# Gate and up of a feed-forward block, from weights stationary to tokens stationary

## The chip, the cores and the metric

One core of a Trainium2 chip runs the whole program. The metric is the device time of one execution in microseconds (us); lower is better. Before the change three timed executions took 2022.8, 2023.21 and 2023.25 us, median 2023.21. A profiled execution beside them took 2023.11 us.

The core has a matrix engine (TensorE, PE in the profile; its weight loads are listed apart as PEld), a vector engine (VectorE, DVE), a scalar engine for activation functions and copies (ScalarE, ACT), GpSimd (POOL) and SyncE (SP), which here does nothing but issue DMAs. Each engine works through its own list of instructions in order, and waits on semaphores where it needs another engine's or a DMA's result. Matrix products accumulate in PSUM banks of 128 partitions x 512 fp32; everything else lies in SBUF.

## What is computed

One sequence of 256 tokens, width 2048, in fp32, passes through two blocks: a sliding-window attention block, and a block with latent attention, differential attention, gates and a feed-forward part. The change touches the feed-forward part, at the end:

```python
h2 = rmsnorm_2(x, ffn_norm_g[i])
x = x + (jax.nn.silu(h2 @ w_ffn_gate[i]) * (h2 @ w_ffn_up[i])) @ w_ffn_down[i]
return rmsnorm_2(x, final_norm_g)
```

`w_ffn_gate` and `w_ffn_up` are 2048 x 5632, `w_ffn_down` is 5632 x 2048.

## The kernel before

**Weights.** All weights lie in HBM as 340 chunks of 16 tiles of 128 x 128, in the order in which the program takes them. SP loads a chunk (1 MB) into one of four buffers `w_raw` (line 53). Half a chunk, 8 tiles, is then cut (lines 79 to 85): ACT casts it to fp32r (`w_hi`), DVE subtracts that from the original (`w_lo`). `w_hi` and `w_lo` have four buffers each. A product is made of three parts: high x high, high x low and low x high. A chunk's load waits until both halves of the chunk four before it have been cut, and a cut until PE is done with the half four before it.

**Two forms of a product.** Activations stand feature-major: 16 tiles `h3_k` of 128 features, each with 256 tokens of high part and 256 of low part side by side. In `gemm` (line 319) a weight tile is stationary and the activations stream: one matmul 512 wide with `w_hi` (high and low part at once, to two halves of a bank), one 256 wide with `w_lo`. The result is feature-major, and its two halves have to be added (`total`, line 387: an ACT copy and a DVE addition). In `gemm_nat` (line 375, with `nat3`, line 367) 128 tokens of an activation tile are stationary and 512 columns of weights stream: three matmuls 512 wide for each of the two token halves, for four weight tiles. The result has the tokens on the partitions, and is complete in one bank. Before the change `gemm_nat` is used for the values of the two attentions (`uv`, `dv`) and for `down`.

**Feed-forward before.** For each of 44 column tiles of gate and of up (lines 958 to 971) `gemm` runs over 16 k. The gate result is multiplied by the tokens' scale `rb` (the reciprocal root mean square, broadcast over the partitions by `rows`, line 282, with a PE matmul), Silu runs on ACT, the up result is multiplied in, and the product is split into `act{m}`, which is the stationary operand of `down`. The first two column tiles of gate and up run interleaved (`gemm4`). `down` then takes `act` in the order of k, 44 of them for each of four column blocks of 512 (the last block has its last eight k held back).

**What runs between.** `after_out` (line 939) is a generator, stepped by `between` after every 16 weight tiles: it makes the scale `r_3`, broadcasts it, and turns the residual `x2` from feature-major to token-major (`x2n`, eight tiles of 128 tokens x 512 features): four PE transposes and one ACT copy per tile (lines 949 to 953). `x2n` is read after the first column block of `down`.

**Buffers and order.** Activations, products and temporaries share one pool, `unit`, of 67 tiles of 128 x 512. A scheduler orders the instructions of each engine ahead of time; a buffer that is given out again makes the new writer wait for the old readers. DMAs of SP, and those of POOL, go round eight completion semaphores each, and a DMA waits for the one eight before it.

Of the kernel before, what the change touches and what calls it, by code (L numbers as in the profile page):

```python
# [9 lines left out]
F32 = mybir.dt.float32  # L10
F32R = mybir.dt.float32r
AF = mybir.ActivationFunctionType
ALU = mybir.AluOpType

P = 128
S = 256
D = 2048
KD = D // P
DFF = 5632
KF = DFF // P  # L20
# [150 lines left out]
def block_kernel(ctx, tc, order, w, x01, xt, bc, fg, cst, out):  # L171
    nc = tc.nc
# [9 lines left out]
    def unit(name, dt=F32):  # L182
        return up.tile([P, 512], dt, name=name, tag="u", bufs=NU)
# [4 lines left out]
    def bank(tag):  # L188
        return psum.tile([P, 512], F32, name=f"ps_{tag}", tag=tag, bufs={"g": 4, "s": 2, "t": 2}[tag])
# [10 lines left out]
    def tt(o, a, b, op):  # L200
        nc.vector.tensor_tensor(out=o, in0=a, in1=b, op=op)  # L201
# [28 lines left out]
    def split_scaled(src, g, hl):  # L230

        hi = hl[:, 0:S]
        if g is None:
            a = nc.scalar.copy(out=hi, in_=src)
            b = nc.vector.tensor_tensor(out=hl[:, S:], in0=src, in1=hi.bitcast(F32), op=ALU.subtract)
        else:
            a = nc.scalar.activation(out=hi, in_=src, func=AF.Copy, scale=g)
            b = nc.vector.scalar_tensor_tensor(out=hl[:, S:], in0=src, scalar=g, in1=hi.bitcast(F32),
                                               op0=ALU.mult, op1=ALU.subtract)
        return a, b  # L240
# [41 lines left out]
    def rows(r, rb=None):  # L282

        dg = unit("diag")[:, 0:S]
        for tb in range(2):
            nc.vector.tensor_scalar(out=dg[:, tb * P:tb * P + P], in0=ident, scalar1=r[:, tb:tb + 1], scalar2=None,
                                    op0=ALU.mult)
        ps = bank("t")
        mm(ps[:, 0:S], ones, dg, True, True)
        if rb is not None:  # L290
            nc.vector.tensor_copy(out=rb, in_=ps[:, 0:S])
        return ps[:, 0:S]
# [26 lines left out]
    def gemm(name, m, acts, tag="g"):  # L319

        ps = bank(tag)
        parts = [(ps, W.take(name, k * P, m * P), acts[k]) for k in range(len(acts))]
        if len(parts) > HALF:
            runs(parts[:HALF], parts[HALF:], HALF)
        else:
            runs(parts, [], len(parts))
        return ps

    def gemm4(name, ms, acts):

        pp = [bank("g"), bank("g"), bank("s"), bank("s")]
        opened = set()
        for k in range(len(acts)):
            parts = [(pp[j], W.take(name, k * P, m * P), acts[k]) for j, m in enumerate(ms)]
            same, other = ("hi", "lo") if k % 2 == 0 else ("lo", "hi")
            run(same, parts, opened)
            run(other, parts, opened)
            between.tiles(len(parts))
        return pp
# [26 lines left out]

    def nat3(o, hl, tb, hi, lo, first, last):

        xh = hl[:, tb * P:tb * P + P]
        xl = hl[:, S + tb * P:S + tb * P + P]  # L370
        mm(o, xh, hi, first, False)
        mm(o, xh, lo, False, False)
        mm(o, xl, hi, False, last)
# [13 lines left out]
    def total(o, ps):  # L387

        nc.scalar.copy(out=o, in_=ps[:, S:])  # L389
        tt(o, o, ps[:, 0:S], ALU.add)  # L390

    def scaled(o, ps, rb):
        total(o, ps)
        tt(o, o, rb, ALU.mult)
# [24 lines left out]
    def transposed(p, on_act=False):  # L419

        ps = bank("t")
        for j in range(3):
            nc.tensor.transpose(out=ps[:, j * P:j * P + P], in_=p[:, j * P:j * P + P], identity=ident)  # L423
        pt = unit("prob_t")[:, 0:384]
        if on_act:
            nc.scalar.copy(out=pt, in_=ps[:, 0:384])
        else:
            nc.vector.tensor_copy(out=pt, in_=ps[:, 0:384])
        return pt


    sq = Squares(8)
# [7 lines left out]
    h = Lazy(KD, first_h)  # L440
# [135 lines left out]
    g = []  # L576
# [348 lines left out]
    h = []  # L925
    for m, ps in blocks("out", 0, 16, mg):
# [5 lines left out]
        split_scaled(t, gcol(G_FFN, m), hl)  # L932
        h.append(hl)
        sq.add(t)
    rb = unit("rb_3")[:, 0:S]
    r_3 = const.tile([P, 2], F32, name="r_3")
    x2n = []

    def after_out():
        yield  # L940
        nc.vector.tensor_copy(out=r_3, in_=rstd(sq.sums(), D))
        yield
        rows(r_3, rb)
        for cb in range(4):
            for tb in range(2):
                yield
                ps = bank("t")
                for i in range(4):
                    nc.tensor.transpose(out=ps[:, i * P:i * P + P], in_=x2[4 * cb + i][:, tb * P:tb * P + P],  # L949
                                        identity=ident)  # L950
                t = unit("x2n")
                nc.scalar.copy(out=t, in_=ps)
                x2n.append(t)

    between.every, between.apart = 16, 1
    between.add(after_out())
    act = []
    for m in range(0, KF):
        if m == 0:
            b4 = gemm4("ffn", [0, KF, 1, KF + 1], h)  # L960
        t = unit("ffn")
        zg, zu = t[:, 0:S], t[:, S:]
        ps = b4[2 * m] if m < 2 else gemm("ffn", m, h)
        scaled(zg, ps, rb)
        nc.scalar.activation(out=zg, in_=zg, func=AF.Silu)
        ps = b4[2 * m + 1] if m < 2 else gemm("ffn", KF + m, h)
        total(zu, ps)
        tt(zu, zu, zg, ALU.mult)
        hl = unit(f"act{m}", F32R)
        split_scaled(zu, None, hl)  # L970
        act.append(hl)
    between.drain()

    tot = sm("tot", 10)
# [82 lines left out]
    return c  # L1057


def _columns(v):  # L1060
    return np.asarray(v, np.float32).reshape(-1, P).T


def _matrices(i):

    pairs = []
    for j in range(16):
        kt = j // 8
        for hd in (16 * kt + j % 8, 16 * kt + 8 + j % 8):
            pairs.extend(range(hd * 64, hd * 64 + 64))  # L1070
    pairs = np.array(pairs)
    in_a, in_2 = i["w_in_a"][0], i["w_in_2"][0]
    uq = i["w_uq_2"][0].reshape(768, 16, 192)
    ukv = i["w_ukv_2"][0].reshape(512, 16, 256)
    kpe = in_2[:, 1280:1344]
    ffn = np.concatenate([i["w_ffn_gate_2"][0], i["w_ffn_up_2"][0]], axis=1)
    return {
        "in_a": np.concatenate([in_a[:, :2048][:, pairs], in_a[:, 2048:2560], in_a[:, 2560:][:, pairs]], axis=1),
        "out_a": i["w_out_a"][0][pairs],
        "in_2": in_2[:, :1280],  # L1080
        "kpe": np.concatenate([kpe, kpe], axis=1),
        "dqk": in_2[:, 1344:5440],
        "dv": in_2[:, 5440:7488],
        "gate": in_2[:, 7488:],
        "uq": np.concatenate([uq[:, :, :128].reshape(768, -1), uq[:, :, 128:].reshape(768, -1)], axis=1),
        "uk": ukv[:, :, :128].reshape(512, -1),
        "uv": ukv[:, :, 128:].reshape(512, -1),
        "mla": i["w_mla_proj_2"][0],
        "diff": i["w_diff_proj_2"][0],
        "out": i["w_out_2"][0],  # L1090
        "ffn": ffn,
        "down": i["w_ffn_down_2"][0],
    }


# [32 lines left out]
```

## Time and profile before

| what | value |
|---|---|
| median of 3 runs | 2023.21 us (2022.8 to 2023.25) |
| profiled execution | 2023.11 us |
| its span, first to last instruction | 2021.3 us |
| TensorE clock granted | 0.999 of full speed |
| PE, PEld, DVE, ACT, POOL busy | 99%, 86%, 65%, 53%, 1% of the span |
| gate and up | 1278.9 to 1773.3 us |
| `down` and the end | 1773.3 to 2021.3 us |

The profile lists groups of instructions as "line engine operation out<-in, shapes, count | busy us, mean ns of one | idle time of the engine ahead of them, and what ended it". Rows of a timeline have start, duration, engine, line, operation and count; the chain of waits has start, duration and what. PE's matmuls are pipelined, so a row's duration is longer than the distance to the next; distances between starts give the rate.

### The profile page before, as it was taken

What the parts mean: (1) busy time and instruction counts of PE and PEld (TensorE: products, weight loads), DVE (VectorE), ACT (ScalarE), POOL (GpSimd) and SP (SyncE); (2) the same over time, 40 slices, a digit from 0 to 9 for tenths busy, and PEclk for the clock granted to TensorE, in tenths of its full rate; (3) what the DMA queues carried; (4) which work ended last, traced back from release to release, by engine and by line L of the source; (5) the groups of instructions that cost most, each with busy time, mean ns of one, the idle gap of its engine ahead of it and who ended that gap; (6) DMA issues with size and microseconds to landing.
All of it is one profiled execution on the core that took longest, in us unless ns stands there. A gap on an engine that the chain in (4) does not pass through costs nothing.

```text
span 2021.3 us, 28390 instructions
## 1 busy us (share of the span) xinstructions
PE 2007.7 (99%) x11338; PEld 1744.3 (86%) x11338; DVE 1309.4 (65%) x2151; ACT 1074.6 (53%) x1821; POOL 18.4 (1%) x25
## 2 busy tenths in 40 slices
PE   9999999999999999999999999999999999999998
PEld 8888888888888888888888888888888888888887
DVE  7778766887857555576665667656666666554544
ACT  6677665756546444455565445554444445444443
POOL 0000000000000000000000000000000000000000
PEclk9999999999999999999999999999999999999999
DMA  8444454444344555545445555455555555555553
GB/s 300 152 144 149 165 209 176 167 149 155 135 169 167 188 188 188 190 167 186 172 166 188 192 196 190 175 179 187 189 188 189 192 191 191 194 209 189 196 197 104
DMA packets 53235, 364.83 MB, mean 180 GB/s; under 512 B 6064, under 2 KB 6576, under 8 KB 9968
## 3 DMA queue, kind: packets, MB, share of 16 engines
q1 hardware_dynamic: 51552, 359.76, 49.8%
q10 hardware_dynamic: 1152, 1.97, 0.3%
q8 instruction: 88, 1.44, 0.3%
q0 software_dynamic: 400, 1.31, 0.2%
q14 instruction: 43, 0.35, 0.1%
HBM read 360.91 MB, written 2.10 MB: 180 GB/s over the span
## 4 chain that ended last, share of the span: by engine, by line
PE 96%; DVE 2%; ACT 1%; issue 1%; DMA 0%; POOL 0%; POOLq 0%; ACTq 0%
PE ps_g L198 88%; PE ps_s L198 5%; PE ps_t L198 2%; PE ps_t L423 1%; DVE rope_t L201 1%; DVE w_lo L85 0%; DVE k_n L201 0%; DVE q_r L201 0%; ACT w_hi L84 0%; DMA x01t<-x 0%; PE ps_t L949 0%; PE ps_t L853 0%; ACT prob L414 0%; PE ps_t L829 0%; DVE prob L408 0%
## 5 line engine op out<-in xcount | busy, mean ns | idle before, releaser
L85 DVE TENSOR_TENSOR w_lo<-w_raw,w_hi 128x1024 fp32r<-128x1024 f32 (+1 forms) x677 | 824.9, 1220 | 296.7 <-ACT w_hi L84 276.3
L84 ACT CAST w_hi<-w_raw 128x1024 fp32r<-128x1024 f32 (+1 forms) x677 | 708.2, 1047 | 352.9 <-PE ps_g L198 269.5
L198 PE MATMUL ps_g<-h,w_hi 128*128 128x512 f32 x3048 | 742.1, 392 | 0.1
L198 PEld LDWEIGHTS ps_g<-h,w_hi 128*128 128x128 f32 x3048 | 558.4, 188 | 111.2 <-issue 3.5
L198 PEld LDWEIGHTS ps_g<-h,w_lo 128*128 128x128 f32 x3048 | 392.1, 191 | 17.8 <-issue 3.2
L198 PE MATMUL ps_g<-h,w_lo 128*128 128x256 f32 x3048 | 404.0, 284 | 0.0
L198 PE MATMUL ps_g<-w_hi,act 128*128 128x512 f32 x688 | 212.1, 389 | 0.0
L198 PEld LDWEIGHTS ps_g<-w_hi,act 128*128 128x128 f32 x688 | 129.1, 188 | 26.9
L389 ACT COPY ffn<-ps_g 128x256 f32<-128x256 f32 x86 | 31.8, 373 | 200.6 <-PE ps_g L198 200.6
L198 PE MATMUL ps_g<-w_lo,act 128*128 128x512 f32 x344 | 133.8, 389 | 0.0
L201 DVE TENSOR_TENSOR ffn<-ffn,ps_g 128x256 f32<-128x256 f32 x86 | 35.8, 420 | 143.9 <-ACT ffn L389 143.9
L198 PE MATMUL ps_g<-w_hi,h 128*128 128x512 f32 x256 | 79.5, 389 | 0.0
L198 PEld LDWEIGHTS ps_g<-w_lo,act 128*128 128x128 f32 x344 | 64.6, 188 | 13.3
L198 PE MATMUL ps_g<-y_m,w_hi 128*128 128x512 f32 x256 | 63.8, 391 | 0.0
L198 PE MATMUL ps_g<-y_d,w_hi 128*128 128x512 f32 x256 | 61.2, 391 | 0.0
L198 PE MATMUL ps_g<-g,w_hi 128*128 128x512 f32 (+1 forms) x240 | 57.8, 377 | 0.0
L198 PEld LDWEIGHTS ps_g<-w_hi,h 128*128 128x128 f32 x256 | 48.0, 188 | 10.0
L198 PE MATMUL ps_g<-mg,w_hi 128*128 128x512 f32 x224 | 56.0, 391 | 0.0
L198 PEld LDWEIGHTS ps_g<-y_m,w_hi 128*128 128x128 f32 x256 | 47.0, 188 | 9.1
L198 PEld LDWEIGHTS ps_g<-y_d,w_hi 128*128 128x128 f32 x256 | 47.0, 188 | 9.1
L198 PE MATMUL ps_g<-c,w_hi 128*128 128x512 f32 x208 | 53.0, 397 | 0.0
L198 PE MATMUL ps_g<-w_lo,h 128*128 128x512 f32 x128 | 49.8, 389 | 0.0
(255 smaller groups left out, 1899.4 us busy)
## 6 DMA issues: line engine op xcount, KB each, us to landing
w_raw<-w SPq DMA_DIRECT2D x337, 1024.0 KB, 4.8
w_raw<-w SPq DMA_DIRECT2D x5, 512.0 KB, 7.6
x_t<-xt SPq DMA_DIRECT2D x7, 256.0 KB, 7.4
fgt<-fg POOLq DMA_DIRECT2D x4, 256.0 KB, 5.5
out<-x2n SPq DMA_DIRECT2D x4, 256.0 KB, 3.1
out<-x2n ACTq DMA_DIRECT2D x4, 256.0 KB, 3.5
x01t<-x SPq DMA_DIRECT2D x1, 310.0 KB, 4.8
w_raw<-w ACTq DMA_DIRECT2D x1, 256.0 KB, 5.0
```

What stands on the lines that cost most here:

```text
L84: a = nc.scalar.copy(out=hi[:, q], in_=src[:, q])
L85: b = nc.vector.tensor_tensor(out=lo[:, q], in0=src[:, q], in1=hi.bitcast(F32)[:, q], op=ALU.subtract)
L198: nc.tensor.matmul(out=o, lhsT=a, rhs=b, start=start, stop=stop, skip_group_check=True)
L201: nc.vector.tensor_tensor(out=o, in0=a, in1=b, op=op)
L389: nc.scalar.copy(out=o, in_=ps[:, S:])
L423: nc.tensor.transpose(out=ps[:, j * P:j * P + P], in_=p[:, j * P:j * P + P], identity=ident)
```

## The change

Gate and up use `gemm_nat`: 11 strips of 512 columns, gate and up of a strip one after the other (64 weight tiles each). A result has 128 tokens x 512 hidden features, while `down` needs the features on the partitions. The new generator `hidden` does this for a strip in three parts:

1. after the gate half: Silu for each of the two token halves, straight from PSUM, with the scale `r_3` as its per-token factor (so `rb` goes);
2. after the up half: the product, a DVE block transpose of the 128 x 512 tile (every 32 x 32 block is turned where it stands), and 16 DMAs on SP (`moved`, new line 434) that carry 32 x 128 quarters, 16 KB each, to other partitions;
3. after the next strip's gate half, so half a strip later: the split into `act_hi` and `act_lo`, which also puts the columns in order.

The residual is turned in the same way: 32 DVE block transposes and 128 such DMAs, issued from POOL. The hidden features, the output columns and the final gain are permuted on the host by `_quarters`, so that the quarters land as whole tiles. The output's columns are put back at the end.

```diff
+    def moved(tr, name, queue):
+        o = unit(name)
+        for a in range(4):
+            for b in range(4):
+                queue.dma_start(out=o[32 * b:32 * b + 32, a * P:a * P + P],
+                                in_=tr[32 * a:32 * a + 32, b * P:b * P + P])
+        return o
...
-        yield
-        rows(r_3, rb)
         for cb in range(4):
             for tb in range(2):
-                yield
-                ps = bank("t")
+                yield 3
+                tr = unit("x2_t")
                 for i in range(4):
-                    nc.tensor.transpose(out=ps[:, i * P:i * P + P], in_=x2[4 * cb + i][:, tb * P:tb * P + P],
-                                        identity=ident)
-                t = unit("x2n")
-                nc.scalar.copy(out=t, in_=ps)
-                x2n.append(t)
+                    nc.vector.transpose(
+                        out=tr.rearrange("p (a m j) -> p a m j", a=4, m=4)[:, :, i, :],
+                        in_=x2[4 * cb + i][:, tb * P:tb * P + P].rearrange("p (a j) -> p a j", a=4))
+                x2n.append(moved(tr, "x2n", nc.gpsimd))
...
-    for m in range(0, KF):
-        if m == 0:
-            b4 = gemm4("ffn", [0, KF, 1, KF + 1], h)
-        t = unit("ffn")
-        zg, zu = t[:, 0:S], t[:, S:]
-        ps = b4[2 * m] if m < 2 else gemm("ffn", m, h)
-        scaled(zg, ps, rb)
-        nc.scalar.activation(out=zg, in_=zg, func=AF.Silu)
-        ps = b4[2 * m + 1] if m < 2 else gemm("ffn", KF + m, h)
-        total(zu, ps)
-        tt(zu, zu, zg, ALU.mult)
-        hl = unit(f"act{m}", F32R)
-        split_scaled(zu, None, hl)
-        act.append(hl)
+    def hidden(pg, pu):
+        parts = []
+        for tb in range(2):
+            z = unit("ffn")
+            nc.scalar.activation(out=z, in_=pg[tb], func=AF.Silu, scale=r_3[:, tb:tb + 1])
+            parts.append(z)
+        yield
+        for tb in range(2):
+            z = parts[tb]
+            tt(z, pu[tb], z, ALU.mult)
+            tr = unit("ffn_t")
+            nc.vector.transpose(out=tr, in_=z)
+            parts[tb] = moved(tr, "ffn_m", nc.sync)
+        yield
+        hls = []
+        for t in parts:
+            t = t.rearrange("p (a g i) -> p g a i", a=4, g=4)
+            hi, lo = unit("act_hi", F32R), unit("act_lo", F32R)
+            nc.scalar.copy(out=hi.rearrange("p (g a i) -> p g a i", a=4, g=4), in_=t)
+            tt(lo.rearrange("p (g a i) -> p g a i", a=4, g=4), t,
+               hi.bitcast(F32).rearrange("p (g a i) -> p g a i", a=4, g=4), ALU.subtract)
+            hls.append((hi, lo))
+        for k in range(4):
+            q = slice(k * P, k * P + P)
+            act.append([(hi[:, q], lo[:, q]) for hi, lo in hls])
+    last = iter(())
+    for u in range(DFF // 512):
+        banks = []
+        work = hidden(gemm_nat("ffn", u * 512, h), banks)
+        for _ in last:
+            pass
+        next(work)
+        banks.extend(gemm_nat("ffn", DFF + u * 512, h))
+        next(work)
+        last = work
+    for _ in last:
+        pass
...
+def _quarters(n):
+    return np.arange(n).reshape(-1, 4, 4, 32).transpose(0, 2, 1, 3).reshape(-1)
```

How the order of instructions moves. First SP's list, in the middle of gate and up. Before, it holds weight loads alone; each waits for the semaphore it reuses and for DVE, which has cut the chunk whose buffer it takes:

```order
L53 DMA w_raw_13051<-w 128x2048 [waits DMAHW4_49,DVE_49]
L53 DMA w_raw_13098<-w 128x2048 [waits DMAHW5_49,DVE_49]
L53 DMA w_raw_13148<-w 128x2048 [waits DMAHW6_49,DVE_49]
L53 DMA w_raw_13195<-w 128x2048 [waits DMAHW7_49,DVE_49]
L53 DMA w_raw_13245<-w 128x2048 [waits DMAHW0_49,DVE_49]
```

Now, at the end of strip 1 (`ffn_t` is the block-transposed tile, `ffn_m` the moved one; `w_raw_13239` holds the first chunk of strip 2's up half, `w_raw_13273` the second):

```order
L53 DMA w_raw_13169<-w 128x2048 [waits DMAHW5_49,DMAHW1_49,DVE_49]
L53 DMA w_raw_13239<-w 128x2048 [waits DMAHW6_49,DMAHW2_49,DVE_49]
L439 DMA ffn_m_13006<-ffn_t_13004 32x128 [waits DVE_49]
L439 DMA ffn_m_13006<-ffn_t_13004 32x128 x3
L439 DMA ffn_m_13006<-ffn_t_13004 32x128 [waits DMAHW3_49]
...
L439 DMA ffn_m_13026<-ffn_t_13024 32x128 [waits DMAHW7_49,DVE_49]
...
L439 DMA ffn_m_13026<-ffn_t_13024 32x128 [waits DMAHW6_49]
L53 DMA w_raw_13273<-w 128x2048 [waits DMAHW7_49,Activation_49]
L53 DMA w_raw_13307<-w 128x2048 [waits DMAHW0_49,DVE_49]
```

Between two weight loads there now stand 32 DMAs, 16 of each token half, once in every strip; between two such blocks there are eight loads.

Second ACT's list in the same stretch. Before, the casts of weights alternate with short steps on 256 columns (`ffn` is gate or up, `act10` a split result):

```order
L84 CAST w_hi_13391<-w_raw_13389 128x1024 [waits DMAHW7_49,PE_49,Activation_49]
L389 COPY ffn_13243<-ps_g_13291 128x256 [waits PE_49]
L84 CAST w_hi_13395<-w_raw_13389 128x1024 [waits Activation_49]
L234 CAST act9_13337<-ffn_13243 128x256 [waits DVE_49]
L84 CAST w_hi_13441<-w_raw_13439 128x1024 [waits DMAHW0_49,PE_49,Activation_49]
L389 COPY ffn_13340<-ps_g_13341 128x256 [waits PE_49]
```

Now, around the end of strip 3's gate half (`act_hi` are the two splits of strip 2, `ffn` the two Silus of strip 3, `w_raw_13611` the first chunk of strip 3's up half, `w_raw_13645` the second; DMASW are POOL's DMAs, DMAHW those of SP):

```order
L84 CAST w_hi_13581<-w_raw_13563 128x1024 [waits DVE_49,PE_49]
L986 CAST act_hi_13597<-ffn_m_13400 128x512 [waits DMAHW4_49,DMAHW5_49,DMAHW3_49,DMAHW6_49,DMAHW2_49,DMAHW7_49,DMAHW1_49,DMAHW0_49]
L84 CAST w_hi_13613<-w_raw_13611 128x1024 [waits DVE_49,PE_49]
L84 CAST w_hi_13629<-w_raw_13611 128x1024 [waits DVE_49,PE_49]
L986 CAST act_hi_13601<-ffn_m_13420 128x512 [waits DMAHW4_49,DMAHW5_49,DMAHW3_49,DMAHW6_49,DMAHW2_49,DMAHW7_49,DMAHW1_49,DMAHW0_49]
L972 ACTIVATE ffn_13605<-ps_g_13437,r_3_12298 128x512 [waits DMASW4_49,DMASW3_49,DMASW5_49,DMASW2_49,DMASW6_49,DMASW1_49,DMASW7_49,DMASW0_49,PE_49]
L972 ACTIVATE ffn_13607<-ps_g_13438,r_3_12298 128x512 [waits PE_49]
L84 CAST w_hi_13647<-w_raw_13645 128x1024 [waits DMAHW7_49,DVE_49]
L84 CAST w_hi_13663<-w_raw_13645 128x1024 [waits DVE_49]
```

A split now waits for SP's quarters, and a Silu for a whole gate half of PE (strips 3 to 6 also for POOL's quarters, whose buffers it takes over); the casts of the second chunk of the up half stand behind them.

More of the change, by code (lines that the diff above doesn't have):

```diff
@@ L367, in nat3 @@
     def nat3(o, hl, tb, hi, lo, first, last):
-        xh = hl[:, tb * P:tb * P + P]
-        xl = hl[:, S + tb * P:S + tb * P + P]
+        if isinstance(hl, list):
+            xh, xl = hl[tb]
+        else:
+            xh = hl[:, tb * P:tb * P + P]
+            xl = hl[:, S + tb * P:S + tb * P + P]
         mm(o, xh, hi, first, False)
@@ L934, in block_kernel @@
         sq.add(t)
-    rb = unit("rb_3")[:, 0:S]
     r_3 = const.tile([P, 2], F32, name="r_3")
@@ L1075, in _matrices @@
     kpe = in_2[:, 1280:1344]
-    ffn = np.concatenate([i["w_ffn_gate_2"][0], i["w_ffn_up_2"][0]], axis=1)
+    ffn = np.concatenate([i["w_ffn_gate_2"][0], i["w_ffn_up_2"][0]], axis=1)[:, _quarters(2 * DFF)]
     return {
@@ L1091, in _matrices @@
         "ffn": ffn,
-        "down": i["w_ffn_down_2"][0],
+        "down": i["w_ffn_down_2"][0][:, _quarters(D)],
     }
@@ L1109 @@
             "sinks_a", "lambda_q1_2", "lambda_q2_2", "lambda_k1_2", "lambda_k2_2")])[None], (P, 1)),
-        "fg": np.tile(i["final_norm_g_2"].reshape(1, D), (P, 1)),
+        "fg": np.tile(i["final_norm_g_2"][_quarters(D)].reshape(1, D), (P, 1)),
         "cst": _constants(),
@@ L1126 @@
     res = _run(nc, [arrays], core_ids=[0])
-    return res.results[0]["out"].reshape(1, S, D)
+    out = np.empty((1, S, D), np.float32)
+    out[0][:, _quarters(D)] = res.results[0]["out"].reshape(S, D)
+    return out
```

## The prediction

> **What bounds the kernel now.** I read the page's busy times first, then the chain that ended last, then the groups of costliest instructions, to see who waits for whom.
>
> ```profile
> PE 2007.7 (99%) x11338; PEld 1744.3 (86%) x11338; DVE 1309.4 (65%) x2151; ACT 1074.6 (53%) x1821; POOL 18.4 (1%) x25
> ...
> PE 96%; DVE 2%; ACT 1%; issue 1%; DMA 0%; POOL 0%; POOLq 0%; ACTq 0%
> ...
> L85 DVE TENSOR_TENSOR w_lo<-w_raw,w_hi 128x1024 fp32r<-128x1024 f32 (+1 forms) x677 | 824.9, 1220 | 296.7 <-ACT w_hi L84 276.3
> L84 ACT CAST w_hi<-w_raw 128x1024 fp32r<-128x1024 f32 (+1 forms) x677 | 708.2, 1047 | 352.9 <-PE ps_g L198 269.5
> ```
>
> TensorE is never idle, and 96% of the chain is its matmuls. Feeding it is not the limit: ACT's idle time ahead of a weight cast is ended by PE (it gives back a `w_hi` buffer), and DVE waits for ACT. So what counts in gate and up is the PE time of a weight tile; everything else counts only when it outlasts the buffers. First PE's rate there, from the PE timeline (old form on gate and up, then the token-stationary form in `dv` on `h`, then in `down`), where the stage begins, and where `act` is first read:
>
> ```profile
> 1278.91 0.61 PE L198 MATMUL ps_g<-h,w_hi 128*128 128x512 f32 x2
> ...
> 1402.16 2.08 PE L198 MATMUL ps_g<-h,w_lo 128*128 128x256 f32 x16
> 1404.07 3.82 PE L198 MATMUL ps_g<-h,w_hi 128*128 128x512 f32 x16
> 1407.72 2.08 PE L198 MATMUL ps_g<-h,w_lo 128*128 128x256 f32 x16
> ```
>
> ```profile
> 588.63 0.62 PE L198 MATMUL ps_g<-w_hi,h 128*128 128x512 f32 x2
> 589.08 0.39 PE L198 MATMUL ps_g<-w_lo,h 128*128 128x512 f32 x1
> ...
> 602.23 0.62 PE L198 MATMUL ps_g<-w_hi,h 128*128 128x512 f32 x2
> ```
>
> ```profile
> 1900.92 0.62 PE L198 MATMUL ps_g<-w_hi,act 128*128 128x512 f32 x2
> ...
> 1901.60 0.62 PE L198 MATMUL ps_g<-w_hi,act 128*128 128x512 f32 x2
> ```
>
> ```profile
> L198 PE MATMUL ps_g<-w_hi,act x688: 389/389/389, 1773.3 to 2007.0; 128*128 128x512 f32 x172
> ```
>
> The old form spends 1407.72 - 1402.16 = 5.56 us on 16 weight tiles (the chain below says 5.57). The other form spends 0.68 us on a group of three matmuls, both on `h` (20 groups from 588.63 to 602.23, 13.60 us) and on `act` (1900.92 to 1901.60); four weight tiles need six of them, 1.36 us, so 16 need 5.44. The old form's 256-wide matmul costs 1.91/16 = 0.119 us, more than half of the 512-wide one's 0.228.
>
> **The change part by part: PE.** The chain of waits in this stage:
>
> ```profile
> 1296.28 0.43 PE ps_t L198 x2
> ...
> 1318.53 0.44 PE ps_t L949 x4
> 1318.97 5.57 PE ps_g L198 x32
> ```
>
> ```profile
> L949 PE MATMUL ps_t<-ident,y x32: 270/272/273, 1302.2 to 1342.7; 128*128 128x128 f32 x32
> ```
>
> - Gate and up, before: 88 strips x 5.57 = 490.2 us. With 8 x 0.44 for the residual's transposes, 0.43 for the row-scale broadcast and 0.34 for the sums of squares this is 494.5, and the rows above give 1773.3 - 1278.91 = 494.4: nothing else is in the stage.
> - After: 11 strips x 2 x 16 k x 2 token halves = 704 groups of three, x 0.68 = 478.7 us: **-11.4**.
> - The 32 transposes leave PE: 8 x 0.44 = **-3.5**. The broadcast leaves it, since the scale is now per token and rides on Silu: **-0.4**. The sums of squares stay.
>
> Together -15.3 us, if nothing new makes PE wait. Execution profiled: 2023.11 us with a span of 2021.3, so 2007.8; the median of the runs shown (2023.21) is 0.1 above, so **2007.9**.
>
> **What must hide the rest.** ACT and DVE lose work: per 512 columns of gate and up four strips' copies, sums, products and splits of 256 columns (20 DVE, 16 ACT instructions) become 6 and 4 of 512 columns. They are idle 38% and 49% of this stretch:
>
> ```profile
> 1303.00:1773.00 470.00, 470.00 (x2714) 415.70 (x2714) 290.99 (x381) 239.32 (x347) 2.00 (x4) 1.00 0.53 187
> ```
>
> So they cost nothing by volume. What is new is latency, on SP: 32 DMAs stand between two weight loads at the end of each up strip. I call that end E, and "a half" the 8 weight tiles of one cast, 2 x 1.36 = 2.72 us of PE; half 1 is the first of the next gate strip. The loads and casts as they are now:
>
> ```profile
> L84 ACT CAST w_hi<-w_raw x168: 1047/1053/1060, 1302.4 to 1769.8; 128x1024 fp32r<-128x1024 f32 x168
> L85 DVE TENSOR_TENSOR w_lo<-w_raw,w_hi x168: 1224/1226/1228, 1303.4 to 1770.8; 128x1024 fp32r<-128x1024 f32 x168
> L53 SPq DMA_DIRECT2D w_raw<-w x84: 327/328/328, 1304.7 to 1770.3; - x84
> ...
> DMA to landing us min/median/max: 4.6/4.7/5.7
> ```
>
> ```profile
> L952 ACT COPY x2n<-ps_t x8: 578/587/588, 1303.3 to 1343.0; 128x512 f32<-128x512 f32 x8
> L983 DVE SCALAR_TENSOR_TENSOR x2n<-ps_g,r,x2n x7: 741/744/750, 1832.9 to 2007.4; 128x512 f32<-128x512 f32 x7
> L201 DVE TENSOR_TENSOR x2n<-x2n,fgt x6: 684/685/686, 1835.6 to 1955.9; 128x512 f32<-128x512 f32 x6
> ```
>
> Casts run four halves ahead of PE, and four chunks of two halves are loaded ahead of the casts. At E the order has the load of halves 9 and 10 issued; the next one, halves 11 and 12, stands behind the 32. PE reaches half 11 at E + 10 x 2.72 = 27.2, its first `w_lo` at 27.4.
>
> The first quarter can go at E + 2.4: two products from PSUM (0.744 each), one transpose, 0.2 for the semaphores. No row shows a block transpose; between 0.59 (ACT's 512-wide copy) and 1.23 (DVE's 1024-wide subtraction) I take 0.69, DVE's own 512-wide instruction. With s us per quarter SP is free at E + 2.4 + 32 s; load 4.7, cast 1.05, subtraction 1.23: `w_lo` of half 11 stands at E + 9.4 + 32 s. PE waits if that is past 27.4, so **s > 0.56**; the stall eats 15.3/11 = 1.4 us per strip at **s = 0.61**. No 16 KB DMA between partitions is in the trace. The rows nearest to s: SP at the start of the kernel, and whole transfers:
>
> ```profile
> 2.60 0.43 SPq L213 DMA_DIRECT2D x_t<-xt  x1
> 3.07 0.66 SPq L53 DMA_DIRECT2D w_raw<-w  x1
> 3.77 0.65 SPq L213 DMA_DIRECT2D x_t<-xt  x1
> ```
>
> ```profile
> out<-x2n SPq DMA_DIRECT2D x4, 256.0 KB, 3.1
> ...
> lam<-bc POOLq DMA_DIRECT2D x1, 256.0 KB, 3.1
> ```
>
> Below: 0.33, SP's time for one issue. Above: 0.70 (3.07 to 3.77, where much larger transfers had filled the queue). Between: 0.47 (2.60 to 3.07), starts that follow each other without a wait. Each quarter also waits for the one eight before it (eight semaphores); landing in 3.1 us that is 0.39 each. I take **0.47**, since 16 KB in 32 rows is less to queue than any of these transfers: SP is free at E + 17.4, half 11 is split at E + 24.4, 3.0 us early. Behind SP stand three more loads, due 5.4 us apart, landing closer; they catch up before the next E.
>
> The second new wait is on ACT: the split of the moved tiles and both Silus stand ahead of the cast of half 11. Second tile landed at E + 2.4 + 15.0 + 3.1 = 20.5, its cast 0.6; Silu waits for the end of half 8, E + 21.8, two of 0.59, then cast and subtraction: 25.3, 2.1 us early. At s = 0.56 the tile lands at 23.4 and the same chain ends at 27.5: the same limit, to 0.1. What waits behind is only the weight casts. The last strip's `act` rows are read 40 k later in `down`, 40 x 1.36 = 54 us of cover.
>
> POOL's 128 quarters: at its own issue they are cheap, but Silu buffers reuse their tiles. By the counts in the program the strictest wait is strip 5's Silu, at 1279 + 5 x 43.5 + 21.8 = 1518, for 112 of them from 1300 on: 1.9 us each would do.
>
> ```profile
> 1771.00 2.17 POOL L978 DMA_DIRECT2D fgt<-fg  x4 [479.39 <-ACT w_hi L84]
> ```
>
> Four 256 KB loads went out in 2.17 us, 0.54 each: hidden, with a factor of three. The residual is read first at 1832.9. [...] No run here shows a POOL DMA beside block transposes.
>
> **The rivals.**
>
> 1. *SP becomes the bound* (slower). s = 0.70: half 11 split at E + 31.8, 4.4 us late, eleven times: +48, so 2056. For it: the two widest issues at the start, and that every quarter carries a wait. Against it: those followed five large transfers; 0.47 before. It decides from s = 0.61. [...]
> 2. *ACT or SP just late* (s between 0.56 and 0.61, or a slow Silu): 0.7 us per strip on average, +8, 2016.
> 3. *POOL starved.* At 3.1 us one after the other (`lam`'s landing) 112 end at 1300 + 347 = 1647, 129 late in one wait: 2137.
> 4. *The form gains nothing on PE*: 2023. Against it: `dv` runs 0.68 in the same form, on `h` tiles of the same shape.
>
> **How the numbers follow.** Forecast 73%; rival 1 16%, rival 2 5%, rival 3 3%, rival 4 3%. Time 2007.9; its own range 2006 to 2011 (the old sum meets the stage to 0.1 us and 0.68 holds over 20 groups, so PE's part is sure to a microsecond or two; a late strip or two adds up to three). The range 2005 to 2032 takes in rivals 2 and 4 and the mild part of rival 1. A difference of 0.2% is about what a measurement of this kernel can tell from no change: below 2019 is faster. Faster 0.77, same 0.04 (rival 4 and the break-even of rival 1), slower 0.19.
>
> **What would show it.** Right: three matmuls per 0.68 us through gate and up, the 32 quarters of one E issued within 15 us, PE without idle time ahead of `w_hi` or `w_lo`, `down` starting near 1758. Wrong: PE idle once per strip, ended by ACT or DVE casts that wait for a load issued late, quarters more than 0.56 us apart on SP; or one long ACT wait for POOL's DMAs. The forecast fails if a quarter takes over 0.6 us, whatever PE gains.

## The result, and the profile after

The changed kernel takes 2056.05 us (median of 4 runs, 2050.16 to 2057.99) against 2023.22 us before: a ratio of 1.0158, 95% interval 1.0136 to 1.018. It is slower by 33 us where the prediction had it 15 us faster. The profiled execution took 2054.36 us, with a span of 2052.4. Gate and up now run from 1278.9 to 1798.4 us, 519.5 us where the sum had 478.7.

The busy times and the engines' shares of the chain that ended last, of the kernel after:

```profile
PE 2015.1 (98%) x10600; PEld 1714.9 (84%) x10600; DVE 1265.7 (62%) x2026; ACT 1034.5 (50%) x1681; POOL 81.3 (4%) x153
...
PE 80%; SPq 9%; DVE 4%; DMA 3%; ACT 2%; issue 2%; POOL 0%; DVEq 0%; POOLq 0%; ACTq 0%
```

Two things stand here. SP's queue, which was not in the chain before, has 9% of it. And PE, with 738 matmuls fewer, is busy 7.4 us longer: it waits, and it also runs slower. The chain between 1400 and 1460 us, one strip, tells the first (start, duration, what):

```profile
1421.16 1.20 DVE ffn L201 x2
1422.36 0.63 DVE ffn_t L979
1424.25 1.26 SPq L439
...
1442.03 0.59 SPq L439
1443.99 5.07 DMA w_raw<-w
1449.13 1.05 ACT w_hi L84
1450.21 1.24 DVE w_lo L85
1451.49 8.52 PE ps_g L198 x29
```

From the end of the up strip (E; PE starts the next strip at 1421.4, and the first token half is complete a little earlier) the path goes through the products, the block transpose, SP's quarters one behind the other, and only then the load of the weights that PE wants next, their cast and their subtraction. SP's own timeline shows the same and gives the price:

```profile
1423.05 20.83 SPq L439 DMA_DIRECT2D ffn_m<-ffn_t  x32
1443.99 22.81 SPq L53 DMA_DIRECT2D w_raw<-w  x8
1471.00 9.38 SPq L439 DMA_DIRECT2D ffn_m<-ffn_t  x15
...
1661.87 20.74 SPq L439 DMA_DIRECT2D ffn_m<-ffn_t  x32
1682.72 21.09 SPq L53 DMA_DIRECT2D w_raw<-w  x8
1708.02 12.43 SPq L439 DMA_DIRECT2D ffn_m<-ffn_t  x19
```

32 quarters take 20.8 us, so **s is 0.65 us**. The groups of these instructions (ns: min/median/max) say that this is the issue itself, 0.59, and hardly a wait:

```profile
L439 SPq DMA_DIRECT2D ffn_m<-ffn_t x352: 507/589/1480, 1325.5 to 1820.7; - x176
L979 DVE STREAM_TRANSPOSE ffn_t<-ffn x22: 700/701/702, 1324.7 to 1801.0; 128x512 f32<-128x512 f32 x22
...
L439 POOL DMA_DIRECT2D x2n<-x_t x128: 498/498/544, 1303.3 to 1442.8; - x128
```

PE's waits in this stage (us in total, times, longest), and the stall of that strip in PE's timeline, with the idle time and its releaser in brackets:

```profile
ACT w_hi L84 <- DMA w_raw<-w: 28.4, 22, 2.2
...
PE ps_g L198 <- ACT w_hi L84: 13.5, 10, 2.0
PE ps_g L198 <- DVE w_lo L85: 7.6, 10, 0.8
```

```profile
1447.66 0.62 PE L198 MATMUL ps_g<-w_hi,h 128*128 128x512 f32 x2
...
1448.34 0.39 PE L198 MATMUL ps_g<-w_hi,h 128*128 128x512 f32 x1
1450.23 0.50 PE L198 MATMUL ps_g<-w_hi,h 128*128 128x512 f32 x1 [1.50 <-ACT w_hi L84]
1451.49 0.50 PE L198 MATMUL ps_g<-w_lo,h 128*128 128x512 f32 x1 [0.76 <-DVE w_lo L85]
...
1453.79 1.05 PE L198 MATMUL ps_g<-w_hi,h 128*128 128x512 f32 x2
...
1455.07 1.05 PE L198 MATMUL ps_g<-w_hi,h 128*128 128x512 f32 x2
```

Before the stall a group of three starts every 0.68 us. Behind it the groups at 1453.79 and 1455.07 are 1.28 us apart. The granted clock shows why; here are the windows behind this stall (the second is the low stretch itself), a low stretch of twice that length in the first strip, and the window behind the stall of 1688, which is 2.05 us long (PE busy, PEld, DVE, ACT and POOL busy, then PEclk, DMA share, GB/s):

```profile
1451.00:1454.00 3.00, 2.51 (x8) 2.03 (x9) 2.17 (x3) 1.80 (x3) 0.00 (x0) 0.76 1.02 431
...
1452.56:1455.97 3.41, 3.41 (x10) 2.65 (x9) 2.37 (x3) 2.00 (x3) 0.00 (x0) 0.50 1.01 425
...
1353.58:1360.41 6.83, 6.07 (x15) 4.76 (x15) 4.25 (x4) 3.36 (x4) 4.31 (x10) 0.50 1.02 419
...
1691.00:1694.00 3.00, 3.00 (x15) 2.48 (x14) 2.60 (x3) 2.28 (x3) 0.00 (x0) 1.00 1.01 429
```

So a strip loses twice: it stands still, and then, behind eight of the eleven stalls (the last is at the start of `down`), runs at half the clock for 3.41 or 6.83 us. SP's rows above give both: strips begin 47.95 us apart at 1423 and 46.15 at 1662, where 64 groups at 0.68 are 43.52.

### The profile page after: what moved, and what is told of

Its sections match the earlier page's. It is cut to its first block, busy times and chain, and to the rows that moved or that the text cites. A ratio compares the mean times of both kernels' runs of the same rounds, so it can differ in the third digit from the quotient of the medians.

```text
span 2052.4 us, 27459 instructions
## 1 busy us (share of the span) xinstructions
PE 2015.1 (98%) x10600; PEld 1714.9 (84%) x10600; DVE 1265.7 (62%) x2026; ACT 1034.5 (50%) x1681; POOL 81.3 (4%) x153
## 4 chain that ended last, share of the span: by engine, by line
PE 80%; SPq 9%; DVE 4%; DMA 3%; ACT 2%; issue 2%; POOL 0%; DVEq 0%; POOLq 0%; ACTq 0%
PE ps_g L198 73%; SPq L439 9%; PE ps_s L198 4%; DMA w_raw<-w 3%; PE ps_t L198 2%; DVE w_lo L85 2%; ACT w_hi L84 1%; PE ps_t L426 1%; DVE rope_t L201 1%; DVE ffn L201 1%; DVE k_n L201 0%; DVE ffn_t L979 0%; DVE q_r L201 0%; PE ps_t L865 0%; ACT prob L417 0%
## 5 line engine op out<-in xcount | busy, mean ns | idle before, releaser
L198 PE MATMUL ps_g<-w_hi,h 128*128 128x512 f32 x1664 | 525.4, 396 | 13.5 <-ACT w_hi L84 13.5
L198 PE MATMUL ps_g<-h,w_hi 128*128 128x512 f32 x1672 | 410.3, 393 | 0.3 <-ACT w_hi L84 0.2
L198 PEld LDWEIGHTS ps_g<-w_hi,h 128*128 128x128 f32 x1664 | 318.1, 191 | 84.3 <-ACT w_hi L84 17.7
L198 PEld LDWEIGHTS ps_g<-h,w_hi 128*128 128x128 f32 x1672 | 306.1, 188 | 63.1 <-issue 3.5
L198 PE MATMUL ps_g<-w_lo,h 128*128 128x512 f32 x832 | 329.7, 396 | 7.6 <-DVE w_lo L85 7.6
L198 PE MATMUL ps_g<-h,w_lo 128*128 128x256 f32 x1672 | 223.2, 284 | 0.0
L198 PEld LDWEIGHTS ps_g<-h,w_lo 128*128 128x128 f32 x1672 | 214.3, 191 | 10.7 <-issue 3.2
L198 PEld LDWEIGHTS ps_g<-w_lo,h 128*128 128x128 f32 x832 | 159.3, 191 | 44.2 <-DVE w_lo L85 10.7
L198 PE MATMUL ps_g<-w_lo,act_hi 128*128 128x512 f32 x344 | 135.2, 393 | 0.8 <-DVE w_lo L85 0.8
L198 PE MATMUL ps_g<-w_hi,act_lo 128*128 128x512 f32 x344 | 135.0, 392 | 0.0
L439 POOL DMA_DIRECT2D x2n<-x_t x128 | 63.0, 498 | 88.2 <-DVE x_t L958 43.5
```

Of the source, the lines that this page charges most:

```text
L198: nc.tensor.matmul(out=o, lhsT=a, rhs=b, start=start, stop=stop, skip_group_check=True)
L439: queue.dma_start(out=o[32 * b:32 * b + 32, a * P:a * P + P], in_=tr[32 * a:32 * a + 32, b * P:b * P + P])
```

## The experiments

**Theory A**: SP issues 32 quarters in 20.8 us, the weight load stands behind them, PE runs dry once a strip, and the clock falls behind the stall. **Theory B**: it is the moved tile's own lateness, through the waits of ACT ahead of the weight casts. **Theory C**: the quarters' traffic, or the DVE, ACT and POOL work around them, disturbs the rest, whoever issues them. **Theory D**: the form is slower over a whole stage than 20 groups showed.

### Both queues: 16 quarters on SP, 16 on POOL

```diff
-            parts[tb] = moved(tr, "ffn_m", nc.sync)
+            parts[tb] = moved(tr, "ffn_m", nc.sync if tb == 0 else nc.gpsimd)
```

> Per strip the first `act` tile's 16 quarters go through SP, the second's through POOL; the whole result is computed. Theory A: SP is free at E + 2.2 + 16 x 0.65 = 12.6, ten us before the point from which PE waits; no stall: 2008 (2005 to 2012). If the price of a quarter rises when two queues issue at once (0.65 x 2 each), nothing is gained over one queue: 2040 to 2056. Theory C: 2045 to 2060.

2008.55 us (2008.42 to 2008.84), ratio to the kernel before 0.9929, interval 0.9914 to 0.9944. All the same quarters are moved, and the 47 us are gone. SP's timeline:

```profile
1411.67 10.64 SPq L439 DMA_DIRECT2D ffn_m<-ffn_t  x16
...
1455.14 10.02 SPq L439 DMA_DIRECT2D ffn_m<-ffn_t  x16
```

These strips are 43.47 us apart; one of ten takes 44.4, with a stall of 0.5. A holds, C and D fall: same traffic, same form, full rate.

### All quarters on POOL

```diff
-            parts[tb] = moved(tr, "ffn_m", nc.sync)
+            parts[tb] = moved(tr, "ffn_m", nc.gpsimd)
```

> The quarters of the `act` tiles are issued by POOL instead of SP; the whole result is still computed. E is the end of an up strip, as in the prediction. Theory A (SP's issue holds the weight loads back: 32 quarters in 20.8 us, 0.65 each, put the next load at E + 23.1, PE then idles 2.2 us per strip and runs at a lower granted clock for some us after each stall): SP is free all the time, PE keeps 0.68 us per group through gate and up, no idle time ahead of `w_hi` or `w_lo`; the sum of the prediction holds: 2008, between 2005 and 2012. Theory C (the quarters' own traffic, or the DVE and ACT work around them, disturbs the weights' loads and casts, whoever issues them): 2045 to 2060 as now. Theory D (the token-stationary form is slower over a whole stage than the 0.68 us read from 20 groups, or draws the clock down by itself): 2030 to 2056, without idle time on PE. POOL still has the residual's quarters until about 1443, so the first two or three strips may wait some us under each theory.

2021.17 us (2018.97 to 2022.11), ratio 0.9989, interval 0.998 to 0.9999. Nine of ten strips up to 1765 us run at 43.5 to 44.0 us, so the loads are on time; one, that of E = 1410, stalls for 4.3 us. There the residual's quarters are still in POOL's queue, and each quarter waits for the one eight before it. The chain of waits in that strip:

```profile
1423.59 5.09 DMA ffn_m<-ffn_t
...
1441.40 1.26 ACT ffn L972 x2
1442.66 0.94 ACT w_hi L84
...
1443.62 1.24 DVE w_lo L85
```

A quarter takes 5.1 us to land here, beside the weight loads (median 4.0 over the kernel, against 1.8 in the changed one), so eight at a time take longer than POOL's 0.50 each. The second tile then comes late, ACT splits it, runs two Silus, and only then casts weights. That is theory B, in one strip. The stall and what follows it are 6.4 us. Another 4 us or so lie after the last piece of the chain, at the program's end; what they are stays open.

### The weight loads on POOL, all quarters on SP

From the kernel with the residual on PE (below):

```diff
-        (queue or self.nc.sync).dma_start(out=t[:, a:b], in_=self.w[c][:, a:b])
+        (queue or self.queue or self.nc.sync).dma_start(out=t[:, a:b], in_=self.w[c][:, a:b])
...
+    W.queue = nc.gpsimd      # for gate and up only
```

> All 32 quarters of a strip stay on SP; the weight loads of gate and up go through POOL instead, and the residual goes through PE's transposes as in the kernel before, so that POOL has nothing else. The whole result is computed. This parts the two ways in which SP's 20.8 us can reach PE. Theory A (only because the weight loads stand behind the quarters on SP): no stall, 2008 + 3.5 for the residual's transposes = 2011.5 (2009 to 2016). Theory B (the moved tile comes late, and ACT's split of it and the Silus stand ahead of the weight casts): the second tile still lands at E + 2.2 + 20.8 + 1.8 = 24.8, its cast 0.62, two Silus 1.2, cast 1.05 and subtraction 1.23 end at E + 28.9 against 27.4 when PE wants the half: 1.5 us late, eleven times, with the clock's drop behind it: 2028 to 2045.

2019.08 us (2018.18 to 2020.08), ratio 0.998, interval 0.997 to 0.9989: between the two. SP's 20 us are all still there, but the loads are past them. PE's waits in gate and up:

```profile
PE ps_g L199 <- DVE w_lo L86: 2.2, 5, 0.8
PE ps_g L199 <- ACT w_hi L85: 0.7, 1, 0.7
```

2.9 us against 21.1 in the changed kernel. In the strip before 1443 the chain of waits is B's: SP's last quarter is issued at 1436.6 and lands in 3.7 us, ACT splits the tile, and only then casts weights. So B is real but small: freed from the queue, the tile's lateness alone costs some 7 us (against 2012.47, the same residual without stalls, below), of which 2.9 are idle time. A is the main cause.

### What an issue costs: fewer and larger, or from HBM

```diff
+        for a in range(4):
+            queue.dma_start(out=o[:, a * P:a * P + P], in_=tr[:, a * P:a * P + P])
```

> Per `act` tile 4 DMAs of 128 partitions x 512 bytes (64 KB) on SP in place of 16 of 32 partitions x 512 bytes (16 KB): the same bytes and the same rows of 512 bytes, a quarter of the DMAs. The quarters are not put to their partitions, so `act` and the output are of other numbers; the work on each engine is that of the changed kernel. If SP's price is per DMA: 8 x 0.6 = 5 us per strip, SP free at E + 7, 2008. If it is per row or byte: 8 x 2.4 = 20 us, 2050 to 2060 as now.

One timed execution: 2007.85 us. The group of these DMAs:

```profile
L447 SPq DMA_DIRECT2D ffn_m<-ffn_t x88: 470/599/1484, 1324.3 to 1765.0; - x88
```

0.60 us for 64 KB, 0.59 for 16 KB: SP's price is per DMA, not per byte or row. This run also gives the account of the loss, since its PE has the same 10600 matmuls: its span is 2005.9 us with PE busy 1992.1. The changed kernel has 46.5 us more, of which 23.0 are PE's busy time (1992.1 to 2015.1) and 23.5 its idle time.

The other run keeps the shape and the count, but half of the DMAs read from HBM:

```diff
+                queue.dma_start(out=o[32 * b:32 * b + 32, a * P:a * P + P],
+                                in_=w[0][32 * a:32 * a + 32, b * P:b * P + P])
...
-            parts[tb] = moved(tr, "ffn_m", nc.sync)
+            parts[tb] = moved(tr, "ffn_m", nc.sync) if tb == 0 else loaded("ffn_m", nc.sync)
```

> Of each strip, the 16 DMAs of the second `act` tile read 32 x 128 pieces of the weights in HBM, in the same shape (32 partitions x 512 bytes), in place of the turned tile in SBUF; the second half of the tokens is then of other numbers. Count, bytes and places in SP's order stay. The whole issue of 0.59 us a DMA against the 0.33 of a 1 MB weight load is what the prediction mis-sized; this asks what makes it dear. If it is the small shape of a DMA, or any DMA at all that is not a whole tile: 0.59 for all 32, 2050 to 2060 as now. If it is the source in SBUF: 16 x 0.33 + 16 x 0.65 = 15.7, SP free at E + 17.9, no stall, 2008.

One timed execution: 2009.56 us. Both kinds side by side:

```profile
L439 SPq DMA_DIRECT2D ffn_m<-ffn_t x176: 512/589/1477, 1324.2 to 1771.3; - x176
L448 SPq DMA_DIRECT2D ffn_m<-w x176: 310/420/1523, 1335.0 to 1779.2; - x176
```

And SP's four 256 KB stores at the end of the changed kernel, from SBUF to HBM:

```profile
L1067 SPq DMA_DIRECT2D out<-x2n x4: 332/335/348, 2041.4 to 2047.3; - x4
```

A DMA of the same size to the same place is queued in 0.42 us when it reads HBM, and in 0.59 when it reads SBUF. Neither answer of the expectation is exact (0.42, not 0.33); the larger part of the difference goes with the source. But a source in SBUF is not dear by itself, since the stores to HBM take 0.34: dear on SP, at 0.59, is a DMA with both ends in SBUF. Why SP needs longer for it, no run shows.

### How many quarters SP can carry

Two runs leave a few of the second tile's last quarters to POOL (`tail` is 1 for that tile):

```diff
-                queue.dma_start(
+                (nc.gpsimd if tail and a == 3 else queue).dma_start(                # 28 on SP
+                (nc.gpsimd if tail and a == 3 and b >= 2 else queue).dma_start(     # 30 on SP
```

> 28 of a strip's 32 quarters on SP, the last four of the second `act` tile on POOL. The whole result is computed. Theory A, now with the sizes that the changed kernel's strips show (quarters from E + 1.95 on, 0.65 us each, a half split 7.5 us after its load is issued, wanted by PE at E + 28.15): load at E + 20.2, split at E + 27.7, 0.4 in time: no stall, 2008 (2006 to 2012). Theory C (any SBUF-to-SBUF traffic of this size beside the weight loads costs the time): 2045 to 2056.

> 30 of 32 quarters on SP, two on POOL; the whole result is computed. Theory A: load at E + 21.5, split at E + 29.0, 0.85 us late; each stall takes another 0.56 us to fill PE's pipeline again, and, in some strips, 1.65 us of half clock: 11 x 1.4 = 15 without the clock, so 2023, and 2018 to 2041 with it. If the limit were not where the prediction's working puts it (32 s = 19.5 us for no gain, that is 30 quarters): 2008 or 2050.

The next has DVE turn the four quarters that keep their partitions straight into place, and leaves SP 24:

```diff
+                if own is not None and a == b:
+                    nc.vector.transpose(out=o[32 * a:32 * a + 32, a * P:a * P + P],
+                                        in_=own[32 * a:32 * a + 32, a * P:a * P + P])
+                    continue
```

> Four of the 16 quarters of each `act` tile keep their partitions (piece a of the partitions to columns a). These are turned by DVE straight into place (8 more DVE instructions of 32x128 per strip) and SP moves only the other 24. The whole result is computed. Theory A: SP is free at E + 2.4 + 0.9 + 24 x 0.65 = 18.9, load 5.1, cast 1.05, subtraction 1.24 end at E + 26.3, 1.1 before PE wants the half: 2008 (2006 to 2012). If the true limit lies lower than the prediction's working has it (25 instead of 27.4), 1 to 1.5 us per strip with the clock's drop: 2025 to 2035.

| quarters on SP per strip | us, median | ratio to before, 95% interval |
|---|---|---|
| 16 | 2008.55 | 0.9929 (0.9914 to 0.9944) |
| 24 | 2008.14 | 0.9926 (0.9911 to 0.9941) |
| 28 | 2012.81 | 0.9948 (0.9933 to 0.9963) |
| 30 | 2026.19 | 1.0013 (1.0003 to 1.0023) |
| 32 | 2056.05 | 1.0158 (1.0136 to 1.018) |

Flat up to a limit, then steep. SP's timelines with 24, and with 30:

```profile
1411.27 15.62 SPq L443 DMA_DIRECT2D ffn_m<-ffn_t  x24
...
1454.74 15.30 SPq L443 DMA_DIRECT2D ffn_m<-ffn_t  x24
```

```profile
1459.97 20.02 SPq L439 DMA_DIRECT2D ffn_m<-ffn_t  x30
...
1505.46 19.75 SPq L439 DMA_DIRECT2D ffn_m<-ffn_t  x30
```

With 28, SP's 18.2 to 18.7 us already cost 4.8 us more than the expectation's 2008, and 0.8 more than its range: three stalls of 0.2 and some tenths without a recorded wait in most strips. With 30 every strip stalls, for 0.75 to 1.6 us.

### The residual back on PE

```diff
-                tr = unit("x2_t")
+                ps = bank("t")
                 for i in range(4):
-                    nc.vector.transpose(
-                        out=tr.rearrange("p (a m j) -> p a m j", a=4, m=4)[:, :, i, :],
-                        in_=x2[4 * cb + i][:, tb * P:tb * P + P].rearrange("p (a j) -> p a j", a=4))
-                x2n.append(moved(tr, "x2n", nc.gpsimd))
+                    nc.tensor.transpose(out=ps[:, i * P:i * P + P], in_=x2[4 * cb + i][:, tb * P:tb * P + P],
+                                        identity=ident)
+                t = unit("x2n")
+                nc.scalar.copy(out=t.rearrange("p (g m j) -> p m g j", m=4, g=4),
+                               in_=ps.rearrange("p (m g j) -> p m g j", m=4, g=4))
+                x2n.append(t)
```

> The residual goes through PE's 32 transposes and ACT's copies as in the kernel before; only gate and up are changed. The whole result is computed. Theory A (SP's issue alone costs the time): the residual's quarters on POOL cost nothing, so this is 8 x 0.44 = 3.5 us slower than the changed kernel: 2056 + 3.5, 2057 to 2063. Theory C (the 128 quarters on POOL and their traffic disturb the first strips): up to 2 us per strip for three strips are won back, 2050 to 2054.

2039.65 us (2036.23 to 2045.3), ratio 1.0084, interval 1.0065 to 1.0104: 16 us faster than the changed kernel, and outside both expectations. Work that PE has more of made the kernel faster. In its first three strips SP is as late as in the changed kernel, but PE's stall is about 1.1 us in place of 2.2 to 2.7, since the transposes keep PE from reaching the late weights so soon. Behind these shorter stalls the clock does not fall, and later it falls behind three of the eight that follow. Two of those later stalls in PE's timeline:

```profile
1585.95 0.50 PE L198 MATMUL ps_g<-w_hi,h 128*128 128x512 f32 x1 [1.55 <-ACT w_hi L84]
1587.20 0.50 PE L198 MATMUL ps_g<-w_lo,h 128*128 128x512 f32 x1 [0.76 <-DVE w_lo L85]
...
1723.27 0.50 PE L198 MATMUL ps_g<-w_hi,h 128*128 128x512 f32 x1 [0.73 <-ACT w_hi L84]
1724.53 0.50 PE L198 MATMUL ps_g<-w_lo,h 128*128 128x512 f32 x1 [0.76 <-DVE w_lo L85]
```

The stall of 2.31 us left the clock at 1.00, and the one of 1.49 brought it to half. So length alone does not decide; the place counts too. The low stretches of one execution stand on a grid: in the changed kernel they start at 1353.58, 1404.78, 1452.56, 1500.35 us and so on, 15 and 14 steps of 3.41 us apart, and last one step or two. These are the steps of this run that hold the two stalls, and the step behind the shorter one:

```profile
1582.39:1585.80 3.41, 2.00 (x9) 1.31 (x7) 0.00 (x0) 1.30 (x2) 0.00 (x0) 1.00 1.01 428
1585.80:1589.21 3.41, 2.51 (x10) 1.88 (x11) 3.15 (x3) 2.92 (x4) 0.00 (x0) 1.00 1.02 430
...
1722.34:1725.75 3.41, 1.92 (x7) 1.21 (x7) 2.36 (x2) 2.90 (x4) 0.00 (x0) 1.00 1.02 432
1725.75:1729.16 3.41, 3.41 (x9) 2.63 (x9) 2.36 (x2) 1.42 (x2) 0.00 (x0) 0.50 1.03 420
```

The longer stall lies across two steps, with PE idle for 1.41 us of one and 0.90 of the other. The shorter lies in one, and the next step runs at 0.50. In the profile of the changed kernel, from 1279 to 1850 us, the six steps at full clock with 1.82 to 1.98 us of idle PE are all followed by a low one, and none with 1.39 or less is; of the four with 1.57, 1.59, 1.62 and 1.63, the second and the fourth are. What decides between those four, no run here shows. A low step costs 1.7 us of PE's time (strips of 46.15 and 47.95 us in the changed kernel, with stalls of 2.05 and 2.26, give 1.6).

So the 16 us are in part luck. The two profiled executions are 12.1 us apart (spans 2052.4 and 2040.3): PE idles 5.7 us less (18.1 for 23.8), and low steps cost 5.1 in place of 17.1, while the transposes take some 4. Of these 12.0 us, 6.8 belong to the first three strips; the rest hangs on the length and the place of the later stalls, which are not the same in every execution (2036.23 to 2045.3 us, at granted clocks of 0.999 to 0.993).

To size the residual's term where no stall hides it, the same edit was made to the kernel that moves 24 quarters:

> The kernel that moves only 24 quarters (the four that keep their partitions are turned in place by DVE), with the residual through PE's 32 transposes as before. The whole result is computed. It sizes the residual's term by itself, where no stall hides it: 8 x 0.44 = 3.5 us more than with the quarters on POOL, 2011.6 (2010.5 to 2012.5). In the changed kernel the same step back made it 16 us faster, which the account explains by the transposes' filling time in which PE would have stood idle in strips 1 to 3, and by fewer drops of the clock. If the residual's quarters on POOL cost something that the account misses: 2008 or less.

2012.47 us (2011.88 to 2012.71) against 2008.14: 4.3 us. The term is real. In the changed kernel PE's transposes would have stood in time in which PE idles anyway.

### No DMA at all: DVE turns and moves the pieces

```diff
-            tr = unit("ffn_t")
-            nc.vector.transpose(out=tr, in_=z)
-            parts[tb] = moved(tr, "ffn_m", nc.sync)
+            o = unit("ffn_m")
+            for a in range(4):
+                for b in range(4):
+                    nc.vector.transpose(out=o[32 * b:32 * b + 32, a * P:a * P + P],
+                                        in_=z[32 * a:32 * a + 32, b * P:b * P + P])
+            parts[tb] = o
```

> No DMA moves the `act` tiles: DVE transposes each of the 16 pieces of 32 x 128 by itself and writes it straight to the other 32 partitions. The whole result is computed. Theory A: SP has only weight loads, which are on time. What is new is DVE: the residual's transposes of 128x128 take 0.22 us each in the changed kernel, so 32 pieces take 7.1 us in place of 2 x 0.70. They stand ahead of the weight subtraction of half 5, due at E + 11.1, and begin at E + 0.8: with the two products they end at E + 9.4, the subtraction at 10.6, in time by half a microsecond: 2008 (2006 to 2012). If a piece costs 0.3 us or more the same subtraction ends 1.4 us late or later, eleven times: 2025 to 2045.

2075.37 us (2074.78 to 2075.79), ratio 1.0258, interval 1.0241 to 1.0275: the slowest of all. The pieces, and PE's waits:

```profile
L981 DVE STREAM_TRANSPOSE ffn_m<-ffn x352: 289/303/310, 1323.8 to 1828.4; 32x128 f32<-32x128 f32 x176
...
1423.01 10.13 DVE L981 STREAM_TRANSPOSE ffn_m<-ffn 32x128 f32<-32x128 f32 x32
...
1434.31 0.88 DVE L958 STREAM_TRANSPOSE x_t<-y 128x128 f32<-128x128 f32 x4
```

```profile
PE ps_g L198 <- DVE w_lo L85: 36.4, 10, 4.3
```

32 pieces of 32x128 take 10.1 us, 0.32 each, and four 128x128 blocks 0.88, 0.22 each. The stall is 3.6 us in most strips, with the clock's drop behind every one. My expectation had the place wrong too: the subtraction that stands behind the pieces is that of the half due 8.4 us after E, not 11.1. The same mistake as the change's, on another engine: a block of small instructions ahead of the one that feeds PE.

## Why the prediction was wrong, step by step

**The step that failed** is "I take 0.47, since 16 KB in 32 rows is less to queue than any of these transfers". It measured 0.65. The rows it was chosen from are all loads from HBM, and the run with pieces from HBM shows that 0.47 was the right price for those: on SP's timeline 16 of them took 7.5 to 8.7 us, 0.47 to 0.54 each. For a DMA from SBUF to SBUF it was not, and its bytes do not count (64 KB: 0.60). 32 x 0.18 = 5.8 us of SP per strip were missing from the sum; the forecast had 3.0 us in hand.

**The frame around it held.** "`w_lo` of half 11 stands at E + 9.4 + 32 s" gives E + 30.2 for s = 0.65; PE took it at 1451.49, E + 30.1 (two small errors cancel: the quarters begin at E + 1.7, not 2.4, with 0.06 us between the transpose's end and the first of them, where the sum has 0.2 for semaphores, which no run shows; and the load and the steps behind it take some 0.6 us longer than taken). The limit from which PE waits, s = 0.56 or 17.9 us of SP, is where the series bends: nothing with 15.6 us, the first tenths with 18.2 to 18.7. And "the stall eats 15.3/11 = 1.4 us per strip at s = 0.61", 19.5 us of SP, is where 30 quarters (19.6 to 20.1 us) come out, at 1.0013 of the time before; that this fits so well is partly chance, since such a strip idles less than 1.4 us on average and loses the rest behind the stall. The two bounds, 0.33 and 0.70, held the value.

**Rival 1 came true**, with 2056 forecast and 2056.05 measured, but half by chance. It took s = 0.70, 4.4 us late eleven times. It was 0.65, and PE idled 23.5/11 = 2.1 us per strip. The other 23.0 us are PE running slower behind the stalls. The two restarts of PE in a stall take 0.6 us per strip beside the idle time (46.15 - 43.52 - 2.05, a strip without a drop), 6.4 in all, and eight low stretches, six of 3.41 us and two of 6.83, take half of their 34.1 us, 17.1; together 23.5. No term of the prediction held that. A stall was priced at its own length, while it cost twice that.

**What was right.** PE's term: strips of 43.5 us without a stall, 64 x 0.68, and two kernels at 2008.1 and 2008.6 for a forecast of 2007.9. The block transpose, 0.70 for an assumed 0.69. POOL: 0.50 per quarter for 0.54, done by 1443 us and never in PE's way, so rival 3 had nothing in it; the issue of a quarter took 0.50 to 0.54 us beside DVE's block transposes, and 0.50 beside its subtractions and with DVE idle. The residual's term: 4.3 us for 3.5. Landing was better than taken, 1.8 us for 3.1, so the ring of eight did not bind on SP (it did on POOL when all quarters went there, where landing was 4 to 5). ACT's chain, given 2.1 us in hand, has none at s = 0.65, as "the same limit, to 0.1" said: the loads alone, taken off SP, left some 7 us.

**The weight of the evidence.** The range gave rival 1 only its mild part. The argument against it, that its 0.70 followed large transfers, was about a row of another kind of DMA, as was the argument for 0.47. With no row of an SBUF-to-SBUF DMA in the trace, and the break-even at 0.61 between bounds of 0.33 and 0.70, an even choice between the ends would have put a chance of about a quarter beyond it, and a range true to that would have held most of rival 1. The time of SP's issue is what decided: half of the quarters on a second engine is worth 47 us (2008.55 against 2056.05).

## What to carry to other kernels

Price the issue of a DMA per DMA, from rows with the same kind of source and destination, and multiply by what stands ahead of the load that feeds the bottleneck: a queue that is idle most of the time can still be the bound for 20 us. Put such bursts on two queues, or make them fewer, before the limit and not at it, since the time is flat up to it and steep beyond; moving 16 or 24 of the 32 quarters on SP beats both kernels (2008.55 and 2008.14 us). Count a short stall of PE at more than its length: here 32 quarters lost 46.5 us for 23.5 of idle time, and 30 quarters 20.5 for 12.8 (spans of 2026.4 and 2005.9 us).

## What the runs showed of the hardware that was not expected

- SP needs 0.59 us to queue a DMA from SBUF to SBUF, 16 or 64 KB alike, against 0.42 for the same piece from HBM, 0.33 for a 1 MB weight load and 0.34 for 256 KB from SBUF to HBM. POOL queues a quarter of the same size in 0.50.
- The granted clock fell to half for one or two steps of a 3.41 us grid behind every step that held 1.82 us or more of idle PE in the changed kernel from 1279 to 1850 us, and behind some with 1.49 to 1.63; a stall of 2.31 us that lay across two steps left it alone.
- More PE work in the right place made the kernel 16 us faster, by shortening three stalls, and in part by where the later stalls fell.
- A quarter on POOL's queue lands in 4.0 us (median, all 32 there), on SP's in 1.8. The landing goes with the weight loads beside it and not with the queue: in the changed kernel POOL's quarters land in 1.6 from 1335.5 to 1343.5, when SP issues no load, and in 3.6 from 1303 to 1322, beside loads; and SP's land in 3.6 with the loads on POOL (medians).
- DVE needs longer for a 32x128 block transpose (0.32 us in a row of them) than for a 128x128 one (0.22).
